# A hybrid layer with a mixture of experts: the sixteen tasks of the embedding gate put into units 4, 6 and 7, and a register read moved from unit 10 to unit 4

## The chip, the core and the metric

The kernel runs on one core of a Trainium2 chip. A core has TensorE (PE; its weight loads are listed apart as PEld), VectorE (DVE), ScalarE (ACT), GpSimd (POOL), SyncE (SP), which here issues all transfers, and 16 DMA engines. Each engine works through its own instructions in their order; semaphores tie them together. The metric is the device time of one execution in microseconds. A kernel's time is the median over its executions; the profile is one further execution with its own time.

## What is computed

One decoder layer on 512 tokens of width 1024, all in float32. Attention, convolution and the first norm lie ahead of the stage that matters here. Behind them comes

```python
ffn = hier_moe(x, w_router_g, b_router_g, w_router_e, b_router_e, w_gate, w_up, w_down)
ple = jax.nn.sigmoid(x @ w_ple_gate) * (p @ w_ple_proj)
x = layer_norm(ALPHA * x + ffn + ple, ln2_g, ln2_b)
```

`hier_moe` sends each token to 2 of 32 experts; an expert is `(silu(xb @ w_gate) * (xb @ w_up)) @ w_down` with two 1024 x 512 matrices and one 512 x 1024. `ple` is the embedding gate: a 1024 x 1024 product, a sigmoid, and a 256 x 1024 projection of `p`.

## The kernel before

**Units.** The experts are sorted by load and handled in twelve units: `KINDS = "PQPPQPPQPPQP"`. A P unit has two experts with 64 token slots each, a Q unit four with 32. A unit has eight gate steps (line 898: one step takes the 128 rows k of gate and up weights), the activation (902 to 904), a transpose of the hidden rows (909, 911), and four down steps (918). The weights come in pieces of 1 MiB, each two half pieces of 512 KB (`load_expert`, line 263); a P unit uses 12 pieces, a Q unit 24, two in each step. All weights are read once, so the stage moves about 200 MB.

**Slots.** All large buffers lie in 24 slots of 1 MiB (`Slots`). `pump` puts the loads of a fixed queue into the program as soon as a slot is free in program order; the instruction on SP waits until the matmuls that read the slot before are done. What other buffers hold, the weights can't use; "pieces ahead" are those issued beyond the step being computed.

**Filler.** Between the weight steps, `pace` fills in other work of TensorE from two lanes: scatters of the previous unit's output (930, eight pairs of matmuls), the selection matrices (890), gathers of the tokens for coming units (764), and the gate's tasks. A list of weights sets the share at each point: in a P unit most of it stands between the last gate step and the first down step; in a Q unit it is spread, with half of it in that place. This place is called a unit's pause below.

**The gate.** Its sixteen tasks are four chunks of 256 output columns (`w_pg`) times four tiles of 128 tokens. A task (`ple_task`) is 24 matmuls of 128 x 256 (132 to 134: the product as three products of rounded halves), two projections (743, two records each), a sigmoid on ACT (753), a product on DVE (754) and an addition on POOL (758). `PLE` says how many tasks a unit gets. The chunk's weights are loaded before the unit of the chunk's first task, and a chore in the unit ahead of it (`ple_chunk`) splits them on ACT and DVE into a pair of slots, which are given back behind the chunk's fourth task. The split token rows (four slots) and the projection's operands (one) are held from unit 2 to the last task.

**The overflow test.** If an expert has more tokens than its slots, a loop at the end of unit 10 handles the rest (`overflow`, line 961 on). Unit 2 counts the blocks into `nxi`; every engine reads the number into a register (961) and branches on it (962). Here nothing overflows. On SP the branch stands behind a wait for all issued loads; the last unit's last two pieces (line 270) are issued only behind it.

Of the kernel before, what the change touches and what calls it, by code (L numbers as in the profile page):

```python
# [19 lines left out]
T = 512  # L20
# [5 lines left out]
NE = 32  # L26
EPG = 8
FE = 512
CAP = 64
# [19 lines left out]
SEL = 1024.0  # L49
N_SLOTS = 24  # L50
WARM = 9
PLE = {4: 4, 6: 1, 7: 5, 9: 1, 10: 5}
WEIGHTS = {"P": [1.5, 0, 1.5, 0] + [5, 2.5] + [0, 1, 0], "Q": [2, 2, 2, 1.5] + [3, 2] + [1, 2, 1]}
LAST = [4, 0, 4, 0, 2, 2]

# [44 lines left out]
def hybrid_moe_layer_kernel(ctx: ExitStack, tc: tile.TileContext, xT, xtok, pT, w_in, w_conv, w_out, ln1, w_r,  # L100
                            b_r, w_e, w_last, w_pg, w_pp, ln2, cst, out):
    nc = tc.nc
# [8 lines left out]
    def ps(tag):  # L111
        return psum.tile([P, 512], F32, tag=tag, name=f"ps_{tag}", bufs=banks[tag])

    def sm(name, shape, dtype=F32, bufs=2):
        return spool.tile(list(shape), dtype, tag=name, name=name, bufs=bufs)
# [37 lines left out]
    def claim(key, shape, dtype=F32, urgent=False):  # L153

        (wants.appendleft if urgent else wants.append)((key, shape, dtype))
# [13 lines left out]
    def need(key):  # L169
        while key not in loaded:  # L170
            pump(slots.left() - 1)
        return loaded.pop(key)
# [72 lines left out]
    tasks = {}  # L245
    for n in sorted(PLE):
        t = sum(len(v) for v in tasks.values())
        tasks[n] = list(range(t, t + PLE[n]))
    rows_of, base = w_e.rearrange("n u p i d -> (n u p i) d"), {}
# [464 lines left out]
    def ple_start():  # L714

        for j in range(2):
            for i in range(2):
                claim((("x", j), i), [P, KD, 2 * P], F32R)
            yield from halve(("x", j), x1T[j])

    def ple_chunk(c):
        for i in range(2):
            claim((("pg", c), i), [P, KD, 256], F32R)
        yield (("pg", c), 1)
        yield from halve(("pg", c), need(("pg", c)))
# [3 lines left out]
    def ple_task(n):  # L729
        c, tt = divmod(n, NT)  # L730
        if n == 0:
            ple["pq"] = need(("pq",))
        pq = ple["pq"].t
        cc, ts = slice(c * 256, (c + 1) * 256), slice((tt % 2) * P, (tt % 2 + 1) * P)
        o = ps("s")
        held_bank[0] = True
        (xh, xl), (gh, gl) = ([b.t for b in ple[key]] for key in (("x", tt // 2), ("pg", c)))
        for k in range(KD):
            mm3(o[:, 0:256], xh[:, k, ts], xl[:, k, ts], gh[:, k], gl[:, k], k == 0, k == KD - 1)
            if k % 2:  # L740
                yield 0.65
        for k in range(2):
            nc.tensor.matmul(o[:, 256:512], pq[:, k * T + tt * P:k * T + (tt + 1) * P], proj_part(pq, c)[:, k],
                             start=(k == 0), stop=(k == 1))
        if tt == 3:
            slots.give(*ple["pg", c])
            if c < 2:
                load_proj(pq, c + 2)
            if c == 3:
                slots.give(ple["pq"], *(b for j in range(2) for b in ple["x", j]))  # L750
        yield 0.4
        s = sm("ps", [P, 256], bufs=1)
        nc.scalar.activation(s, o[:, 0:256], AF.Sigmoid)  # L753
        nc.vector.tensor_mul(s, s, o[:, 256:512])  # L754
        held_bank[0] = False
        yield 0.2
        r = row(tt)[:, cc]
        nc.gpsimd.tensor_tensor(r, r, s, op=ALU.add)  # L758
        yield 0.01
# [182 lines left out]
    nxi = cpool.tile([P, 1], I32, name="nxi")  # L942

    def find_blocks(keys):
        for b in range(1, NBLK):
            nc.vector.tensor_scalar(keys[:, b - 1], cnt, float(CAP * (b - 1)), None, op0=ALU.is_gt)

    def count_blocks():

        o = ps("z")  # L950
        for tt in range(NT):
            nc.tensor.matmul(o[:, 0:NE], onesb, mc[:, tt], start=(tt == 0), stop=(tt == NT - 1))
        nc.vector.tensor_sub(cnt, o[:, 0:NE], caps)
        keys = sm("hw", [P, FE], bufs=1)[:, 0:(NBLK - 1) * NE].rearrange("p (b e) -> p b e", e=NE)
        find_blocks(keys)
        nx = sm("nx", [P, 1])
        nc.vector.tensor_reduce(nx, keys, axis=AX.XY, op=ALU.add)
        nc.vector.tensor_copy(nxi, nx)

    def overflow():  # L960
        nv = nc.values_load(nxi[0:1, 0:1], min_val=0, max_val=2 * T // CAP + NE)
        with tc.If(nv > 0):
            own = list(slots.q)
            ws, wb, tb, kb = own[0:4]
# [1 line left out]
            n = (NBLK - 1) * NE  # L966
# [81 lines left out]
    def add(cost, gen, lane=1):  # L1048
        lanes[lane].append((cost, gen))
# [22 lines left out]
    def fill(share):  # L1072

        spare[0] += share * (rest(0) + rest(1))
        while (lanes[0] or lanes[1]) and spare[0] > 0:
            spare[0] -= any_piece()
        spare[0] = min(spare[0], 1.0)

    def drain():
        while lanes[0] or lanes[1]:  # L1080
            any_piece()
# [15 lines left out]
    def place_pair(n):  # L1097
        places[n] = t = sm("pt", [P, T], F32R, bufs=1)
        e, m, cap = UNITS[n]
        place(t, lambda tt: rmb[:, tt, e:e + m], m, cap)  # L1100
        yield 0.3
# [13 lines left out]
    for n in range(NU):  # L1115
        g, r = GROUP_OF[n]
        ne, cap = UNITS[n][1:]
        o = [ps("mm") for _ in range(2)]
        point = [0]

        def pace():
            w = (LAST if n == NU - 1 else WEIGHTS[KINDS[n]])[point[0]:]
            if w[0]:
                fill(w[0] / sum(w))
            point[0] += 1

        def pieces(u):
            return [need(("e", n, j, u)) for j in range(ne // 2)]

        if scat is not None:  # L1130
            add(3.6, scat, 0)
        add(0.3, place_pair(n), 0)
        done[:] = [0.0, 0.0]
        ahead = n == GROUPS[g][-1] and g + 1 < NG
        if ahead:
            claim(("xe", g + 1), [P, KD, GROUP], F32, True)
            if g % 2:
                claim(("pts", g + 1), [P, NT, 2 * GROUP], F32R, True)
        for t in tasks.get(n, []):
            add(3.5, ple_task(t))  # L1140
        if n + 2 == min(tasks):
            chores.append(ple_start())
        for t in tasks.get(n + 1, []):
            if t % NT == 0:
                chores.append(ple_chunk(t // NT))
        chore()
        for k in range(KD):
            bs = pieces(k)
            gate_up(o, k, [xe[g].t[:, k, r * P + i * cap:r * P + (i + 1) * cap] for i in range(ne)],
                    [b.t[:, i] for b in bs for i in range(2)])  # L1150
            slots.give(*bs)
            if n == NU - 1 and k == 1:
                closed.clear()
                slots.q.rotate(-4)
            serve()
            if k == 1 and ahead:
                select(g + 1)
                add(7.7 if len(GROUPS[g + 1]) > 1 else 5.3, gather_group(g + 1))
            if k > 0:
                chore()  # L1160
            if n == 0 and k == 2:
                late[0] = group_weights(0)
                next(late[0])
            if r == 0 and k == 4:
                for _ in late.pop(g):
                    pass
            if n == 2 and k == 6:
                count_blocks()
            if k % 2:
                pace()  # L1170
        h = sm("hw", [P, FE], bufs=1)
        swiglu(h, o, wsl[g][r], P)
        pace()
        ht = turn_hidden(h, P)
        pace()
        if n == NU - 1:
            drain()
            break
        o = [ps("y") for _ in range(2)]
        if n == 0:  # L1180
            for j in range(2):
                claim(("acc", j), [P, 2, D])
        for f in range(4):
            bs = pieces(8 + f)
            down(o, f, ht, [b.t[:, i] for b in bs for i in range(2)], cap)
            slots.give(*bs)
            if f == 3:
                claim("y", [P, 4 * T], F32R, True)
            serve()
            chore()  # L1190
            if f < 3:
                pace()
        y = grab("y")
        if n == NU - 2:
            overflow()
            closed.discard(("e", NU - 1, 0, 10))
            serve()
        for h in range(2):
            split_out(halves(y.t, h), o[h], P)
        scat = scatter_pair(n, y.t, y)  # L1200
        while chore():
            pass
        if n == NU - 2:
            drain()
        if n == GROUPS[g][-1]:
            drain()
            slots.give(xe.pop(g))

    n, y, sq, diag = NU - 1, slots.take([P, 4 * T], F32R), slots.take([P, 512]), slots.take([P, 2, P])
# [228 lines left out]
```

## Time and profile before

| | us |
|---|---|
| three executions | 794.64, 796.34, 797.72 |
| median | 796.34 |
| the profiled execution, its own time | 794.04 |
| its span | 792.3 |
| PE busy (share of the span) | 748.8 (95%) |
| DVE, ACT, POOL busy | 315.2, 163.0, 84.3 |
| bytes moved | 233.51 MB, mean 295 GB/s |

The span is what the profile shows from the first to the last instruction; 1.7 us of the execution's time lie around it. A matmul's end is modelled, so TensorE's busy share says little on whether it sets the pace; the bandwidth in slices and what SP waits for say more. The last gate step of each unit and the first down step behind it are found in the timeline of PE by their lines, 898 and 918.

### The profile page before, as it was taken

The numbers are of one execution on the slowest core, as the hardware profiler recorded it, in microseconds if no ns is written. First come the engines' busy times: TensorE is split into PE (matmuls) and PEld (weight loads), VectorE is DVE, ScalarE is ACT, GpSimd is POOL, SyncE is SP. The second block draws the span as 40 slices with busy tenths as digits, with TensorE's granted clock in tenths as the row PEclk, the third lists the DMA queues.
The fourth block names the chain that finished last, engine by engine and source line by source line (L and its number), as shares of the span: only waits on it lengthen the run. The fifth ranks groups of instructions, "written<-read, shape, count | busy, mean of one in ns | idle before, by whom it ended". The sixth has DMA issues, their size and how long they took to land. (4 is left out here: it accounts for less than half of the span.)

```text
span 792.3 us, 11610 instructions
## 1 busy us (share of the span) xinstructions
PE 748.8 (95%) x4322; PEld 445.2 (56%) x4323; DVE 315.2 (40%) x637; ACT 163.0 (21%) x337; POOL 84.3 (11%) x107
## 2 busy tenths in 40 slices
PE   8999999999978999899999999999999999999795
PEld 5887877888857452246334653364454634457242
DVE  3646544646695413445430324241123324012145
ACT  5545454232022020012100120110000111001024
POOL 0224254000142000000000100000000000000005
PEclk9999999999995799999999999999999999999997
DMA  8401301547810779999999999989999999999942
GB/s 310 191 1 31 130 1 54 213 160 302 342 45 1 286 299 356 409 409 405 408 409 408 409 406 410 409 352 335 409 408 407 412 408 408 408 409 408 354 161 106
DMA packets 63675, 233.51 MB, mean 295 GB/s; under 512 B 7040, under 2 KB 10752, under 8 KB 59264
## 3 DMA queue, kind: packets, MB, share of 16 engines
q1 hardware_dynamic: 63616, 232.74, 75.0%
q8 instruction: 35, 0.57, 0.3%
q14 instruction: 24, 0.20, 0.1%
HBM read 230.62 MB, written 2.10 MB: 294 GB/s over the span
## 5 line engine op out<-in xcount | busy, mean ns | idle before, releaser
L898 PE MATMUL ps_mm<-big,big 128*32 128x512 f32 (+1 forms) x1024 | 225.4, 608 | 14.3 <-DMA big<-in_w_e_dram 8.5
L898 PEld LDWEIGHTS ps_mm<-big,big 128*32 128x32 f32 (+1 forms) x1024 | 60.1, 124 | 152.2 <-issue 93.0
L132 PE MATMUL ps_mm<-big,big 128*128 128x512 f32 (+1 forms) x272 | 103.2, 379 | 3.1 <-ACT big L118 2.6
L133 PE MATMUL ps_mm<-big,big 128*128 128x512 f32 (+1 forms) x272 | 100.2, 368 | 0.0
L134 PE MATMUL ps_mm<-big,big 128*128 128x512 f32 (+1 forms) x272 | 99.8, 367 | 0.1
L918 PE MATMUL ps_y<-big,ht 128*32 128x512 f32 (+1 forms) x480 | 86.4, 598 | 0.9 <-DMA big<-in_w_e_dram 0.9
L939 DVE TENSOR_TENSOR big<-big,ps_s 128x512 f32<-128x512 f32 x80 | 52.7, 683 | 82.0 <-PE ps_s L930 81.5
L119 DVE TENSOR_TENSOR big<-big,big 128x512 fp32r<-128x512 f32 (+1 forms) x78 | 63.3, 843 | 37.6 <-ACT big L118 28.6
L118 ACT CAST big<-big 128x512 fp32r<-128x512 f32 (+1 forms) x78 | 54.5, 743 | 50.2 <-DVE big L429 20.1
L758 POOL TENSOR_TENSOR big<-big,ps 128x256 f32<-128x256 f32 x16 | 11.7, 733 | 461.5 <-DVE big L939 266.2
L930 PE MATMUL ps_s<-big,pt 128*128 128x512 f32 x176 | 59.2, 437 | 1.4 <-DVE big L939 0.8
L132 PEld LDWEIGHTS ps_mm<-big,big 128*128 128x128 f32 x272 | 51.8, 190 | 15.3 <-ACT big L118 3.7
L134 PEld LDWEIGHTS ps_mm<-big,big 128*128 128x128 f32 x272 | 51.7, 190 | 8.9 <-DVE big L119 0.4
L133 PEld LDWEIGHTS ps_mm<-big,big 128*128 128x128 f32 x272 | 51.7, 190 | 8.1 <-DVE big L119 0.5
L764 PEld LDWEIGHTS ps_s<-big,big 128*128 128x128 f32 x384 | 48.9, 189 | 10.4 <-issue 6.6
L764 PE MATMUL ps_s<-big,big 128*128 128x256 f32 (+1 forms) x384 | 52.3, 284 | 0.1
L918 PEld LDWEIGHTS ps_y<-big,ht 128*32 128x32 f32 (+1 forms) x480 | 22.7, 122 | 44.7 <-issue 35.7
L371 POOL TENSOR_SCALAR big<-big,rden 128x128 f32<-128x128 f32 (+3 forms) x32 | 39.1, 1232 | 71.1 <-DVE rden L369 71.1
L930 PEld LDWEIGHTS ps_s<-big,pt 128*128 128x128 f32 x176 | 29.4, 192 | 27.9 <-issue 17.3
L754 DVE TENSOR_TENSOR ps<-ps,ps_s 128x256 f32<-128x256 f32 x16 | 6.7, 421 | 90.3 <-ACT ps L753 90.3
L132 PE MATMUL ps_s<-big,big 128*128 128x256 f32 x128 | 37.3, 292 | 0.2
L133 PE MATMUL ps_s<-big,big 128*128 128x256 f32 x128 | 36.1, 282 | 0.0
(234 smaller groups left out, 736.9 us busy)
## 6 DMA issues: line engine op xcount, KB each, us to landing
big<-in_w_e_dram SPq DMA_DIRECT2D x360, 512.0 KB, 10.2
big<-in_w_e_dram SPq DMA_DIRECT2D x12, 1024.0 KB, 8.9
big<-in_w_in_dram SPq DMA_DIRECT2D x11, 1024.0 KB, 6.8
big<-in_w_out_dram SPq DMA_DIRECT2D x4, 1024.0 KB, 6.9
big<-in_w_pg_dram SPq DMA_DIRECT2D x4, 1024.0 KB, 11.1
big<-in_xtok_dram SPq DMA_DIRECT2D x2, 1024.0 KB, 6.9
out_dram<-big SPq DMA_DIRECT2D x8, 256.0 KB, 2.1
big<-in_xT_dram SPq DMA_DIRECT2D x3, 512.0 KB, 8.8
```

The lines of the kernel that those rows point to most:

```text
L118: nc.scalar.copy(hi, raw)
L119: nc.vector.tensor_sub(lo, raw, hi.bitcast(F32))
L132: nc.tensor.matmul(o, ah, bh, start=first, stop=False)
L133: nc.tensor.matmul(o, ah, bl, start=False, stop=False)
L134: nc.tensor.matmul(o, al, bh, start=False, stop=last)
L371: nc.gpsimd.tensor_scalar(pr[h][:, 0:ks], pr[h][:, 0:ks], rden[:, h:h + 1], None, op0=ALU.mult)
L758: nc.gpsimd.tensor_tensor(r, r, s, op=ALU.add)
L764: nc.tensor.matmul(o[:, 0:n], src[tt // 2].t[:, tt % 2, k * P:(k + 1) * P], pt(tt), start=(i == 0), stop=(i == 2 * NT - 1))
L898: nc.tensor.matmul(o[a][i * m:(i + 1) * m], x, w[:, a * FE:(a + 1) * FE], start=(k == 0), stop=(k == KD - 1))
L918: nc.tensor.matmul(o[h][r], ht[:, f, r], w[:, h * 512:(h + 1) * 512], start=(f == 0), stop=(f == 3))
L930: nc.tensor.matmul(o, pt[0:m, tt * P:(tt + 1) * P], y[i][0:m], start=(i == 0), stop=(i == 1))
L939: nc.vector.tensor_add(r, r, o)
```

## The change

Before, units 4, 6, 7, 9 and 10 have 4, 1, 5, 1 and 5 tasks; now units 4, 6 and 7 have 7, 1 and 8. The register read for the overflow test is made behind the third gate step of unit 4, on all engines; the branch stays where it is.

```diff
-PLE = {4: 4, 6: 1, 7: 5, 9: 1, 10: 5}
+PLE = {4: 7, 6: 1, 7: 8}
...
+    over = []
+
     def overflow():
-        nv = nc.values_load(nxi[0:1, 0:1], min_val=0, max_val=2 * T // CAP + NE)
+        nv = over[0]
         with tc.If(nv > 0):
...
             if n == 2 and k == 6:
                 count_blocks()
+            if n == 4 and k == 2:
+                over.append(nc.values_load(nxi[0:1, 0:1], min_val=0, max_val=2 * T // CAP + NE))
```

By the chunks: chunk 1 (tasks 4 to 7) is now loaded with chunk 0 ahead of unit 4 and split in unit 3 instead of 5; chunks 2 and 3 are loaded together ahead of unit 7 and both split in unit 6, where before chunk 3 came in unit 9. The queue of loads is otherwise the same, and no byte is added.

On ACT, unit 4 before, from the rounding of unit 3's output (924) to that of unit 4's. Each row of 753 closes one task, 902 stands behind the last gate step, 911 ahead of the first down step:

```order
L924 CAST big_3352<-ps_y 128x512 x2
L753 ACTIVATE ps<-ps_s 128x256 x3
L902 ACTIVATE hw<-ps_mm 128x512
L753 ACTIVATE ps<-ps_s 128x256
L911 COPY ht<-ps_z 128x512
L766 COPY big_3367<-ps_s 128x256 x4
L808 COPY w_3830<-ps_z 4x128 x2
L924 CAST big_3849<-ps_y 128x512 x2
```

In the change, the same stretch:

```order
L924 CAST big_3354<-ps_y 128x512 x2
L753 ACTIVATE ps<-ps_s 128x256
L1172 TENSOR_LOAD nxi
L753 ACTIVATE ps<-ps_s 128x256 x3
L902 ACTIVATE hw<-ps_mm 128x512
L753 ACTIVATE ps<-ps_s 128x256 x2
L911 COPY ht<-ps_z 128x512
L753 ACTIVATE ps<-ps_s 128x256
L766 COPY big_3369<-ps_s 128x256 x4
L808 COPY w_3940<-ps_z 4x128 x2
L924 CAST big_3959<-ps_y 128x512 x2
```

Between 902 and 911 two tasks are closed where one was, and another one behind 911, where there were only gathers (766).

On SP, ahead of unit 4's first weights, before (241 and 238 are the projection's operands, 148 the gate chunk, 260 and `ISA` work out the address of an expert):

```order
L263 DMA big_2837<-in_w_e_dram 128x1024
L241 DMA big_2840<-in_pT_dram 128x1024
L238 DMA big_2840<-in_w_pp_dram 128x2x256 x2
L148 DMA big_2872<-in_w_pg_dram 128x2048
L260 TENSOR_LOAD table
L260 ISA x2
L263 ISA
```

In the change:

```order
L263 DMA big_2837<-in_w_e_dram 128x1024
L241 DMA big_2840<-in_pT_dram 128x1024
L238 DMA big_2840<-in_w_pp_dram 128x2x256 x2
L148 DMA big_2872<-in_w_pg_dram 128x2048
L148 DMA big_2934<-in_w_pg_dram 128x2048
L260 TENSOR_LOAD table
L260 ISA x2
L263 ISA
```

A second chunk stands ahead of unit 4's weights and takes a slot from them.

## Rows read from the trace of the kernel before

**Rows 1.** The page, bandwidth in 40 equal slices of the span

```profile
GB/s 310 191 1 31 130 1 54 213 160 302 342 45 1 286 299 356 409 409 405 408 409 408 409 406 410 409 352 335 409 408 407 412 408 408 408 409 408 354 161 106
```

**Rows 2.** Table by stretch: us, length, five engines' busy time, clock, DMA share, GB/s

```profile
350.00:515.00 165.00, 159.09 (x868) 74.74 (x868) 51.96 (x106) 22.00 (x40) 2.93 (x4) 1.00 1.03 408
...
530.00:545.00 15.00, 15.00 (x106) 8.55 (x107) 4.95 (x8) 3.07 (x8) 0.00 (x0) 1.00 0.72 247
545.00:700.00 155.00, 151.07 (x874) 74.80 (x869) 39.09 (x80) 13.72 (x28) 5.35 (x8) 1.00 1.03 409
700.00:735.00 35.00, 34.68 (x272) 23.06 (x270) 7.81 (x16) 3.98 (x11) 2.71 (x4) 1.00 1.03 408
```

**Rows 3.** SP's waits, 509 to 546 us: total, times, longest

```profile
SPq L263 <- PE ps_s L930: 8.0, 1, 8.0
SPq L263 <- PE ps_mm L898: 6.8, 4, 2.3
```

**Rows 4.** SP's waits from 700 to 738 us, the same columns

```profile
SPq L263 <- DMA big<-in_w_e_dram: 18.2, 24, 1.3
```

**Rows 5.** Timeline of PE at unit 6's pause: start, length, instruction, count

```profile
522.49 1.89 PE L898 MATMUL ps_mm<-big,big 128*64 128x512 f32 x8
524.30 0.73 PE L930 MATMUL ps_s<-big,pt 128*128 128x512 f32 x2
524.88 1.10 PE L764 MATMUL ps_s<-big,big 128*128 128x256 f32 x8
525.81 0.63 PE L930 MATMUL ps_s<-big,pt 128*128 128x512 f32 x2
...
535.54 1.51 PE L918 MATMUL ps_y<-big,ht 128*64 128x512 f32 x6
```

**Rows 6.** Timeline of PE at unit 4's pause, with one whole task

```profile
443.63 1.90 PE L898 MATMUL ps_mm<-big,big 128*32 128x512 f32 x10 [0.23 <-DMA big<-in_w_e_dram]
...
448.33 0.28 PE L132 MATMUL ps_s<-big,big 128*128 128x256 f32 x1
...
451.21 1.03 PE L743 MATMUL ps_s<-big 128*128 128x256 f32 x4
451.88 1.28 PE L930 MATMUL ps_s<-big,pt 128*128 128x512 f32 x4
...
457.18 1.92 PE L918 MATMUL ps_y<-big,ht 128*32 128x512 f32 x16
```

**Rows 7.** Timeline of PE at unit 7's pause

```profile
578.75 1.91 PE L898 MATMUL ps_mm<-big,big 128*32 128x512 f32 x10 [0.24 <-DMA big<-in_w_e_dram]
...
590.40 1.92 PE L918 MATMUL ps_y<-big,ht 128*32 128x512 f32 x16
```

**Rows 8.** Timeline of PE at the end of unit 10

```profile
733.04 1.92 PE L918 MATMUL ps_y<-big,ht 128*32 128x512 f32 x16
740.29 1.97 PE L898 MATMUL ps_mm<-big,big 128*64 128x512 f32 x4 [5.33 <-PEq L962]
```

**Rows 9.** Timeline of SP, the last piece of unit 10 and what follows

```profile
718.31 1.47 SPq L263 DMA_DIRECT2D big<-in_w_e_dram  x2
```

**Rows 10.** DMA issues from 717.7 to 718.5 us: count, KB, us to landing

```profile
big<-in_w_e_dram SPq DMA_DIRECT2D x2, 512.0 KB, 7.8
```

**Rows 11.** Line 961 and line 962, PE's sequencer: min, median, max ns, start

```profile
L961 PEldq TENSOR_LOAD <-nxi x1: 488/488/488, 733.1 to 733.1; - x1
...
L962 PEldq COMPARE_BRANCH  x1: 6172/6172/6172, 733.7 to 733.7; - x1
```

**Rows 12.** Line 263, all weight loads but the last unit's end

```profile
DMA to landing us min/median/max: 3.2/10.2/13.0
```

**Rows 13.** Line 270, the last unit's loads, ns and first and last start

```profile
L270 SPq DMA_DIRECT2D big<-in_w_e_dram x8: 372/374/392, 738.8 to 756.4; - x8
```

**Rows 14.** DMA issues from 756.3 to 756.7 us

```profile
big<-in_w_e_dram SPq DMA_DIRECT2D x1, 512.0 KB, 7.8
```

**Rows 15.** Timeline of PE, the last unit's last down step

```profile
770.56 1.08 PE L1230 MATMUL ps_mm<-big,ht 128*64 128x256 f32 x8
```

## The prediction

> **What bounds the kernel now.** I read the page's slices first, for the stage in which the weight transfers run without a break. The bandwidth line stands at 400 to 412 GB/s in nearly all slices from the 16th on, with a dent to 352 and 335 and a fall at the end [rows 1]. The table by stretch puts the dent between 530 and 545 us: 247 GB/s there, against 408 and 409 before and behind it [rows 2]. So the expert stage is a stream of weight pieces at 1.049 MB / 408 GB/s = 2.57 us each, and it lost 15 x (1 - 247/408) = 5.9 us once. The waits of SP say why: in that stretch it waited 8.0 and 6.8 us for matmuls, that is, for buffers (slots) that TensorE had not yet freed [rows 3], while from 700 to 738 us it waited 18.2 us for the queue itself, which was full [rows 4]. The TensorE rows at unit 6 show the cause: between the last gate step (522.49 + 1.89 = 524.38) and the first down step (535.54) stand 11.2 us of filler, scatters and gathers [rows 5], and in that time no weight buffer comes free.
>
> The stage ends otherwise. The last piece of unit 10 is issued at 718.31 [rows 9] and such issues land after 7.8 us [rows 10], at 726.1. With the last down step behind it (1.92 us [rows 8]) unit 10 could end at 728.0; it ends at 733.04 + 1.92 = 734.96. TensorE is **7.0 us late** on the stream there. Then it stands still until 740.29 [rows 8], since its branch at the overflow test takes 6.17 us [rows 11].
>
> **The change, part by part.** Nothing is computed less. One gate task is 24 matmuls at (451.21 - 448.33)/24 = 0.12 us plus an end of 451.88 - 451.21 = 0.67 us, 3.55 us in all [rows 6]. Five of them (17.8 us) leave unit 10 and one leaves unit 9; three more go to unit 4 and three more to unit 7.
>
> *Slots.* Splitting a gate chunk makes a pair of buffers that stay until the chunk's fourth task. Before, chunk 1 is split in unit 5; now, with seven tasks in unit 4, in unit 3. Of 24 slots unit 4 held 17 (normalised rows 4, running sum 2, gathered inputs 2, selection 1, expert output 1, gate operand 4, projection 1, one pair 2), so two pieces were in use and five ahead. With a second pair it is three ahead.
>
> *Unit 4's pause.* Before, it runs from 443.63 + 1.90 = 445.53 to 457.18, 11.65 us [rows 6]; the order now has 78 task matmuls in it instead of 36, four ends instead of two, 8 gather matmuls instead of 24. With a gather of eight at 525.81 - 524.88 = 0.93 us [rows 5] that is 11.65 + 42 x 0.12 + 2 x 0.67 - 2 x 0.93 = 16.2 us. The stream has three pieces ahead, two that the last gate step frees, and two from chunk 0's pair: 7 x 2.57, and 0.6 us for a projection reload, 18.6 us. From the landing of the last gate piece to the first new bytes pass 1.9 (gate step) + 16.2 + 1.9 (first down step) + 1.9 us (the shortest issue to landing, 3.2 us [rows 12], less 1.3 us of transfer) = 21.9 us. **Dry: 3.3 us** at least. Unit 6 lost 5.9 us for a longest wait of 8.0, so wait less 2.1 us; here SP would wait from about 3.5 us into the pause (chunk 0's fourth task ends 6 x 0.12 + 0.67 = 1.4 us into it, and four half pieces go out behind that) to 16.2 + 1.9 = 18.1, which is 14.6 us, and lose 12.5 by that. Unit 4 enters with a full queue, unit 6 did not, so I stay near the floor: 6.0 (3.3 to 12.5). The same count on the old unit 4 (nine pieces, 23.1 us, against 17.4) gives no gap, and the trace has none. Between unit 4's gate steps there are now up to 4.9 us of filler (30 task matmuls, an end and a scatter of 524.88 - 524.30 = 0.58 us [rows 5]) with three pieces ahead: 1.5 us (0 to 2.5).
>
> *Unit 6.* Its filler stays. But chunk 3's raw weights now lie in a slot through its first gate steps, and chunk 3's pair takes the next two slots freed behind the last one, while chunk 1's pair comes free a little earlier. One piece more ahead would give 2.57 us back; a piece that waits for the first down step instead of the last scatter costs 2.8 us, and one fewer ahead 2.57 more. I take +3.0 (-2.6 to +5.4), the upper half, because SP's 6.8 us of short waits fall where a slot is now missing.
>
> *Unit 7.* The pause was 590.40 - (578.75 + 1.91) = 9.74 us [rows 7]; 30 matmuls and an end more make 14.0. Eight pieces (four ahead, two that the last gate step frees, two from a finished pair) last 20.6 us, needed are 1.9 + 14.0 + 1.9 + 1.9 = 19.7: no gap by the count, and with unit 4's excess (6.0 - 3.3) added, about 2.0 (0 to 4).
>
> *Units 8 to 10.* Here the gate's seven to nine slots are free, so 12 to 16 pieces are ahead and the stream doesn't break. It ends 6.0 + 1.5 + 3.0 + 2.0 = **12.5 us later** (0.7 to 24 with every bound at its end; 5 to 19 as I believe them).
>
> *The end.* Unit 10 without tasks waits for its weights, so TensorE's 7.0 us of lateness are gone: the unit ends 12.5 - 7.0 = 5.5 us later, and 0.5 us less by the register read that no longer stands ahead of the branch [rows 11]. On SP the overflow test lets everything land before the last four half pieces go out; the last goes at 756.4 [rows 13] and lands 7.8 us later [rows 14], at 764.2. Now that is 776.7, while TensorE wants it at 770.56 [rows 15] + 5.0 = 775.6. So the stream and not TensorE sets the end, by 776.7 - 770.56 = 6.1, **+6.2 us** with the 0.1 us from landing to matmul. The profiled execution of 794.04 us becomes 800.2, and on the median, which is 2.3 us above it, 796.34 + 6.2 = 802.5.
>
> *The register read in unit 4* costs nothing: 0.49 us on TensorE [rows 11] where it waits for weights, and its source was written in unit 2. If that cover were gone it is at most 0.5 us once. Left out: between 0 and 0.5.
>
> [...] The row shows the branch at 6.17 us and the read ahead of it at 0.49 [rows 11], so what is long is the jump and not the value. [...]
>
> **The rivals.** *The slots suffice (no change).* The stream loses only a few us more: unit 4 at its floor and unit 6 with a slot won. At 6 us lost the sum is 6 - 6.3, 796.0. For it: the count gives only 3.3 us for certain. Against: unit 6 of before lost 5.9 us with four pieces ahead.
>
> *The last units win (faster).* Place: the end of unit 10; price: up to 7.0 us of lateness, which vanish whatever happens. It decides if the stream loses under 2.3 us more: with 1 us it is 796.34 - 5.3 = 791.0. For it: unit 6's own gap could shrink by 2.6. Against: a pause of 16.2 us with 18.6 us in hand.
>
> *The early read takes the branch's stall away.* That would give 5.33 us back: 802.5 - 5.3 = 797.2, no change. It would need the jump to be known before it is reached. Against it is the row above: the read ended 0.1 us before the branch began and the wait is the branch's. A chance of 4 in 100.
>
> That the change does nothing is excluded by the order: the tasks stand where its numbers say.
>
> **How the numbers follow.** About 0.5%, 4 us, is what a measurement of this kernel can tell from no change. Slower by more needs a stream that loses over 10.3 us: forecast, 66 in 100, with 802.5. Between: 21 in 100 (17 for the slots, 4 for the branch). Faster: 13 in 100. The range runs from 795 (5 us lost) to 809 (19 us lost).
>
> **What would show it.** In the profile after: a new dent of bandwidth near 460 us, at unit 4's pause of about 16 us, with a long SP wait for matmuls; the dent of unit 6 still there, some 10 us later; a small one at unit 7; 408 GB/s from then on; TensorE waiting for weights in unit 10 and hardly any lateness at its end; the branch still at some 6 us. I am wrong if the bandwidth near 460 us holds, or if unit 6's dent is gone.

## The result, and the profile after

The changed kernel takes 801.21 us (median of seven executions, 800.5 to 804.86) against 795.9 us for the kernel before (also seven); the ratio is 1.0079, with a 95% interval of 1.0058 to 1.01. It is slower, by some 0.8%. The profiled execution took 800.5 us, its span 798.7 us; before they were 794.04 and 792.3.

The page's bandwidth in 40 slices, after; the line of before is in [rows 1]:

```profile
GB/s 305 191 1 50 109 1 54 212 158 316 366 3 1 311 319 367 408 408 408 408 409 373 406 309 404 412 346 294 409 409 351 409 408 409 408 410 408 404 214 105
```

One dent has become four: 373 and 309 GB/s (unit 4), 346 and 294 (unit 6), 351 (unit 7). Behind them 408 to 410, as before. The table by stretch says how much that is. Its columns are the stretch, its length, the busy time of PE, PEld, DVE, ACT and POOL, TensorE's granted clock, the DMA share and GB/s. First before:

```profile
420.00:480.00 60.00, 58.55 (x376) 30.94 (x370) 14.35 (x23) 7.09 (x15) 2.93 (x4) 1.00 1.03 408
480.00:560.00 80.00, 76.50 (x405) 36.05 (x405) 23.87 (x45) 8.67 (x17) 0.73 (x1) 1.00 0.97 377
560.00:640.00 80.00, 78.55 (x483) 42.46 (x484) 21.88 (x47) 8.07 (x19) 3.67 (x5) 1.00 1.03 408
```

and after:

```profile
420.00:460.00 40.00, 39.40 (x270) 26.67 (x269) 7.45 (x14) 3.11 (x8) 4.43 (x6) 1.00 1.01 390
460.00:480.00 20.00, 20.00 (x177) 13.53 (x177) 4.08 (x8) 2.65 (x9) 0.74 (x1) 1.00 0.83 309
480.00:560.00 80.00, 74.32 (x376) 35.19 (x375) 27.64 (x49) 11.76 (x21) 0.73 (x1) 0.96 0.95 364
560.00:640.00 80.00, 79.31 (x526) 46.49 (x527) 17.84 (x41) 6.41 (x14) 5.89 (x8) 1.00 1.01 395
640.00:740.00 100.00, 94.47 (x526) 38.89 (x525) 26.54 (x51) 9.03 (x21) 0.00 (x0) 1.00 1.03 409
```

A stretch lost its length times (1 - GB/s / 409). Before, that is 0.1 + 6.3 + 0.2 = 6.6 us between 420 and 640 us. After, it is 40 x 19/409 = 1.9 between unit 4's gate steps, 20 x 100/409 = 4.9 at its pause (460 to 480 us), 80 x 45/409 = 8.8 around unit 6 and 80 x 14/409 = 2.7 at unit 7: 18.3 us, **11.7 more**. From 460 to 480 us TensorE is busy throughout, at a granted clock of 1.00, while the stream stands still for a quarter of the time: in the pause the engine works, but on filler. The pieces issued ahead carry the stream almost to the pause's end; the standstill itself lies at that end and just behind it (330, 23 and 203 GB/s in the 2 us from 462, 464 and 466).

The clock's 0.96 around unit 6 comes from one place. TensorE waited 3.45 us for weights there, then the granted clock is 0.50 from 510 to 515 us (0.85 in the 5 us behind them), and fifteen matmuls of a gate step take 6.8 us where sixteen later ones take 3.65. What this adds to unit 6's loss no run separates.

SP's waits in two of the stretches of after, first 440 to 475 us (total, times, longest), then 598 to 616 us:

```profile
SPq L263 <- PE ps_y L918: 9.3, 2, 8.7
SPq L263 <- PE ps_mm L898: 5.3, 2, 5.0
...
SPq L263 <- PE ps_y L918: 6.9, 2, 6.2
```

In both, SP's longest wait is for the first down step (918) to free a slot; at the old dent it waited for matmuls too [rows 3]. TensorE's own rows give the pauses, unit 4's and then unit 7's, each from the last gate step to the first down step:

```profile
445.89 1.90 PE L898 MATMUL ps_mm<-big,big 128*32 128x512 f32 x10 [0.23 <-DMA big<-in_w_e_dram]
...
463.97 1.92 PE L918 MATMUL ps_y<-big,ht 128*32 128x512 f32 x16
...
590.65 1.90 PE L898 MATMUL ps_mm<-big,big 128*32 128x512 f32 x10 [0.23 <-DMA big<-in_w_e_dram]
...
606.43 1.92 PE L918 MATMUL ps_y<-big,ht 128*32 128x512 f32 x16
```

That is 463.97 - 447.79 = 16.2 us (11.65 before [rows 6]) and 606.43 - 592.55 = 13.9 us (9.74 before [rows 7]).

The end of unit 10 after, from its last gate step to its last down step, the branch, and the first step of unit 11:

```profile
717.00 1.90 PE L898 MATMUL ps_mm<-big,big 128*32 128x512 f32 x10 [0.24 <-DMA big<-in_w_e_dram]
...
736.19 1.05 PE L918 MATMUL ps_y<-big,ht 128*32 128x512 f32 x2 [0.22 <-DMA big<-in_w_e_dram]
737.47 1.90 PE L918 MATMUL ps_y<-big,ht 128*32 128x512 f32 x10 [0.23 <-DMA big<-in_w_e_dram]
744.14 4.53 PE L898 MATMUL ps_mm<-big,big 128*64 128x512 f32 x10 [4.77 <-PEq L964]
```

Before, the same last gate step began at 706.03 and the last down step stood there without a wait [rows 8]. Now the down steps wait for weights. From the last gate row to the start of the branch pass 737.51 - 717.00 = 20.5 us, where it was 733.66 - 706.03 = 27.6. The chain of waits that ended last (start, length, what) runs through a transfer near its end, that of the very last half piece; before, the chain of the last unit has no transfer in it:

```profile
766.86 8.14 DMA big<-in_w_e_dram
775.00 0.04 issue
775.04 1.08 PE ps_mm L1234 x6
```

### The profile page after: what moved, and what is told of

Same layout as the page of the kernel before. It is cut to its first block, busy times and chain, and to the rows that moved or that the text cites. A ratio compares the mean times of both kernels' runs of the same rounds, so it can differ in the third digit from the quotient of the medians.

```text
span 798.7 us, 11590 instructions
## 1 busy us (share of the span) xinstructions
PE 747.7 (94%) x4323; PEld 443.5 (56%) x4323; DVE 315.7 (40%) x637; ACT 163.6 (20%) x337; POOL 84.4 (11%) x107
## 5 line engine op out<-in xcount | busy, mean ns | idle before, releaser
L898 PE MATMUL ps_mm<-big,big 128*32 128x512 f32 (+1 forms) x1024 | 222.0, 614 | 17.6 <-DMA big<-in_w_e_dram 12.6
L898 PEld LDWEIGHTS ps_mm<-big,big 128*32 128x32 f32 (+1 forms) x1024 | 58.3, 125 | 154.6 <-issue 98.1
L918 PE MATMUL ps_y<-big,ht 128*32 128x512 f32 (+1 forms) x480 | 90.6, 613 | 1.4 <-DMA big<-in_w_e_dram 1.4
L132 PEld LDWEIGHTS ps_mm<-big,big 128*128 128x128 f32 x272 | 51.3, 189 | 16.2 <-ACT big L118 4.8
L764 PEld LDWEIGHTS ps_s<-big,big 128*128 128x128 f32 x384 | 49.4, 189 | 11.6 <-issue 7.4
L758 POOL TENSOR_TENSOR big<-big,ps 128x256 f32<-128x256 f32 x16 | 11.8, 737 | 362.1 <-DVE ps L754 186.3
L132 PE MATMUL ps_s<-big,big 128*128 128x256 f32 x128 | 37.4, 292 | 0.0
L925 DVE TENSOR_TENSOR big<-ps_y,big 128x512 fp32r<-128x512 f32 (+1 forms) x24 | 15.7, 677 | 52.9 <-ACT big L924 52.5
```

The lines of the kernel that those rows point to most:

```text
L132: nc.tensor.matmul(o, ah, bh, start=first, stop=False)
L764: nc.tensor.matmul(o[:, 0:n], src[tt // 2].t[:, tt % 2, k * P:(k + 1) * P], pt(tt), start=(i == 0), stop=(i == 2 * NT - 1))
L898: nc.tensor.matmul(o[a][i * m:(i + 1) * m], x, w[:, a * FE:(a + 1) * FE], start=(k == 0), stop=(k == KD - 1))
L918: nc.tensor.matmul(o[h][r], ht[:, f, r], w[:, h * 512:(h + 1) * 512], start=(f == 0), stop=(f == 3))
L925: nc.vector.tensor_sub(y[1][0:m], o[0:m], y[0][0:m].bitcast(F32))
```

## The experiments

Their results are ratios to the kernel before, run between them on the same chip, with 95% intervals.

**The read alone.**

```diff
 (kernel before)
+            if n == 4 and k == 2:
+                over.append(nc.values_load(nxi[0:1, 0:1], ...))
...
-        nv = nc.values_load(nxi[0:1, 0:1], ...)
+        nv = over[0]
```

> The kernel before with only the register read moved from unit 10 to unit 4. Theory: the read was never late and the 6.17 us behind the branch's row are not its doing, so the time stays within -0.6 to +0.3 us of the 795.9 us before, and the COMPARE_BRANCH row of TensorE's sequencer still lasts 6.0 to 6.3 us. Rival: the read next to the branch is what makes the branch slow; then the branch's row shrinks below 1 us, and TensorE, whose unit 11 begins that much earlier, ends up to 5.3 us sooner (down to 790.6 us, less if the last transfers then bind).

Measured: 794.73 against 795.32 us, 0.9992 (0.9977 to 1.0007). TensorE's branch:

```profile
L964 PEldq COMPARE_BRANCH  x1: 6062/6062/6062, 731.2 to 731.2; - x1
```

The branch takes what it took next to the read [rows 11]. The read is no part of the result, and the rival of the early read falls.

**The table alone.**

```diff
-PLE = {4: 4, 6: 1, 7: 5, 9: 1, 10: 5}
+PLE = {4: 7, 6: 1, 7: 8}
```

> The changed kernel's table (7 tasks in unit 4, 1 in unit 6, 8 in unit 7) with the register read left in unit 10. Theory: the table is the whole of the change, so the time is that of the changed kernel, 801.2 us, within 0.6 us (the read's 0.49 us on TensorE comes back next to the branch), +5.3 to +5.9 us over the kernel before, and the same stretches without traffic at 460 to 475, 525 to 555 and 605 to 620 us. Rival: the early read, with TensorE's halt of 0.49 us in the middle of unit 4, takes part in the dry spell there; then this kernel is more than 1.5 us faster than the changed one.

Measured: 802.19 us, 1.0078 (1.0056 to 1.01), where the whole change has 1.0079. By the medians it is 6.9 us over the kernel before, where 5.3 to 5.9 were expected; by the ratios the two agree. The table is the change, and the rival (the early read takes part in the dry spell) falls.

**Unit 4's part alone.**

```diff
-PLE = {4: 4, 6: 1, 7: 5, 9: 1, 10: 5}
+PLE = {4: 7, 6: 1, 7: 2, 9: 1, 10: 5}
```

> The kernel before with three tasks moved from unit 7 to unit 4 (7, 1, 2, 1, 5 in units 4, 6, 7, 9, 10) and the read as before: unit 10 keeps its five tasks. Theory (lost stream time sets the end): unit 4's pause grows to 16 us, the weight stream falls dry there for 4 to 7 us, unit 6's old dry spell grows by up to 3 us and unit 7's pause shrinks below the old 9.7 us; of some 6 us lost in all, the time grows by 3.5 to 5.6 us (799.4 to 801.5). Rival (TensorE's work in unit 10 sets the end, whatever the stream does): the five tasks still stand in unit 10, so the time stays within 1 us of 795.9.

Measured: 798.0 us, 1.0033 (1.0021 to 1.0045), +2.7 us. The table by stretch of this kernel:

```profile
420.00:480.00 60.00, 59.41 (x439) 40.35 (x441) 11.52 (x22) 5.67 (x15) 5.17 (x7) 1.00 0.94 357
480.00:560.00 80.00, 77.92 (x430) 37.01 (x422) 25.88 (x48) 9.75 (x19) 0.73 (x1) 1.00 1.03 408
560.00:640.00 80.00, 76.92 (x413) 34.00 (x414) 20.53 (x43) 6.21 (x14) 1.46 (x2) 1.00 1.02 409
```

Unit 4 loses 60 x 52/409 = 7.6 us, by itself. The rival (unit 10's work decides, whatever the stream does) falls: five tasks stand in unit 10 and the time still grows. But the expectation of 3.5 us and more was missed, because unit 6, which was to lose more, lost **nothing** (480 to 560 us). Its pause is as long as ever, 11.6 us. What differs is that chunk 1 is finished in unit 6 and chunk 3 is not split until unit 9, so one pair of slots is held in unit 6's pause and not two. This pointed to slots more than any run before it. The loss in these three stretches is only some 1.1 us more than before, less than the 2.7 us of time. Unit 10's last gate row starts 1.9 us later and the way from it to the branch is 0.8 us longer (the table below); from 700 to 740 us this kernel's stream moves 395 GB/s for 408, with SP waiting 3.5 us for a task of unit 10 (2.7 before). What made that end longer stays open.

**Everything into unit 7.**

```diff
-PLE = {4: 4, 6: 1, 7: 5, 9: 1, 10: 5}
+PLE = {4: 4, 6: 1, 7: 11}
```

> The kernel before with unit 9's and unit 10's six tasks moved to unit 7 (4, 1, 11 in units 4, 6, 7) and the read as before. Theory (what counts is how many tasks stand in one unit's pause and how many slots are free there): unit 4 stays as it was, with no dry spell, unit 7's pause grows to 18 to 20 us, the stream loses 20 to 25 us there and at unit 6's place, and the time grows by 9 to 16 us (805 to 812), more than the changed kernel's +5.3, though nothing stands in unit 10 either. Rival (a task costs the same wherever it stands ahead of unit 10, so only their sum counts): about the changed kernel's time, 801.2 within 1.5 us.

Measured: 809.37 us, 1.0171 (1.0149 to 1.0193), +14 us. The rival (a task costs the same wherever it stands) falls. From 480 to 640 us:

```profile
480.00:560.00 80.00, 72.85 (x347) 33.39 (x346) 25.66 (x46) 10.77 (x19) 0.73 (x1) 0.96 0.87 330
560.00:640.00 80.00, 78.30 (x543) 52.15 (x544) 17.34 (x41) 6.46 (x15) 8.09 (x11) 1.00 0.93 352
```

Most of the loss, 80 x 79/409 = 15.5 us, is not at unit 7, where the tasks are, but around unit 6, whose filler is unchanged: there chunks 1, 2 and 3 now hold three pairs.

**Unit 10's tasks made light.**

```diff
 (kernel before, ple_task)
-            mm3(o[:, 0:256], ..., k == 0, k == KD - 1)
+            if n < 11 or k == 0:
+                mm3(o[:, 0:256], ..., k == 0, n >= 11 or k == KD - 1)
```

> The kernel before with unit 10's five gate tasks cut to 3 of their 24 main matmuls each (the gate's sums over 7 of 8 slices of the width are left out there, 5 x 21 x 0.12 = 12.6 us of TensorE); loads, slots and order stay. Theory: TensorE was 7.0 us late at unit 10's end, and what bounds it after that is the stream, whose last half piece is issued at 756.4 us and lands some 13 us later; so only a part of the 12.6 us comes back, 5 to 7 us (789 to 791). Rival 1: TensorE is the bound to the end, then the whole 12.6 us come back (783). Rival 2: the stream bound already, then the time stays within 1 us.

Measured: 790.98 us, 0.9936 (0.9916 to 0.9955), 4.4 us by the medians, 5.1 by the ratio. Both rivals fall: neither all 12.6 us come back, nor none. The size is at the lower end or just under it. (The expectation lets the last half piece land 13 us after its issue. The row says 7.8 [rows 14], at 764.2, some 6.4 us ahead of the last down step, so the range of 5 to 7 us stands.) TensorE's wait in the last unit, which the kernel before doesn't have, says what binds then:

```profile
PE ps_y L1231 <- DMA big<-in_w_e_dram: 2.1, 2, 1.2
```

**The same tasks, a shorter pause.**

```diff
 (the changed kernel, weights of a unit of four experts)
-"Q": [2, 2, 2, 1.5] + [3, 2] + [1, 2, 1]
+"Q": [3, 3, 3, 2] + [2, 1] + [2, 3, 2]
```

> The changed kernel with other weights for the units of eight experts (3, 3, 3, 2 for the gate-up steps, 2, 1 around the turn, 2, 3, 2 for the down steps, in place of 2, 2, 2, 1.5, 3, 2, 1, 2, 1): the same tasks in the same units, but more of each unit's extra work between its steps and less of it in its pause. Theory (the pause in which no weight slot is given back is what runs the stream dry): pauses of units 4 and 7 shrink by 3 to 5 us, the dry spells there by as much, and the time falls by 4 to 8 us against the changed kernel (793 to 797). Rival (the amount of work per unit counts, not where in the unit it stands): no change, 801.2 within 1 us.

(This expectation and those further down call the units of two and four experts units of four and eight. The old list puts 6.5 of its 16.5 parts into the pause of a unit of four experts, two fifths and not half of the filler; the new one 5 of 21.)

Measured: 794.14 us, 0.9988 (0.9971 to 1.0004): some 7 us less than the changed kernel, back at the time before. The rival (the amount of work per unit counts, not its place) falls. Unit 4's pause falls from 16.2 to 9.7 us. The table, 420 to 460, 460 to 480, and unit 7:

```profile
420.00:460.00 40.00, 39.73 (x278) 27.34 (x277) 7.04 (x13) 3.38 (x8) 4.42 (x6) 1.00 0.98 368
460.00:480.00 20.00, 20.00 (x176) 13.56 (x176) 4.08 (x8) 2.19 (x6) 0.73 (x1) 1.00 1.03 408
600.00:640.00 40.00, 40.00 (x266) 23.47 (x263) 12.80 (x27) 3.81 (x9) 2.22 (x3) 1.00 1.03 408
```

The pause of unit 4 loses nothing now; between the gate steps 4.0 us are lost where it was 1.9. What was taken out of the pause was partly given back there, and still 7 us were won.

**The same tasks and pauses, more slots.**

```diff
 (the changed kernel; one rounded half of the gate's operands)
-            for i in range(2):
-                claim((("x", j), i), [P, KD, 2 * P], F32R)
+            claim((("x", j), 0), [P, KD, 2 * P], F32R)
...
-            mm3(o[:, 0:256], xh[:, k, ts], xl[:, k, ts], gh[:, k], gl[:, k], k == 0, k == KD - 1)
+            mm3(o[:, 0:256], xh[:, k, ts], xh[:, k, ts], gh[:, k], gh[:, k], k == 0, k == KD - 1)
```

> The changed kernel with the gate's low halves left out of its operands (the high halves are used in their place, so that every task keeps its 24 matmuls and its duration; the gate's rounding is coarser, and VectorE's subtractions for the low halves are gone): 2 slots in place of 4 for the tokens and 1 in place of 2 for each chunk of the gate's weights, 3 to 4 slots more for the weight stream in units 4 to 7. Theory (slots held by the gate's operands are why the stream can't run through the longer pauses): the pauses stay at 16 and 14 us, but the dry spells at 460 to 475, 525 to 555 and 605 to 620 us shrink from 16.3 us together to under 5, and the time falls by 10 to 18 us against the changed kernel (783 to 791). Rival (the stream stalls for what stands in the way of its issue or transfer, not for slots): the dry spells stay and the time is within 2 us of 801.2.

Measured: 786.41 us, 0.9884 (0.9865 to 0.9904), nearly 15 us under the changed kernel. The pauses of units 4, 6 and 7 are the same, 16.2, 11.6 and 13.9 us, and the stream doesn't break:

```profile
420.00:480.00 60.00, 59.40 (x445) 39.91 (x445) 11.88 (x23) 6.62 (x17) 5.17 (x7) 1.00 1.03 408
480.00:560.00 80.00, 79.55 (x461) 41.10 (x456) 24.17 (x48) 11.04 (x21) 1.46 (x2) 1.00 1.03 409
560.00:640.00 80.00, 79.72 (x538) 48.47 (x538) 21.80 (x47) 8.12 (x19) 5.16 (x7) 1.00 1.03 408
```

TensorE does the same number of matmuls in the same places; with three to four slots more, 0.3 us are lost of the 18.3. (The kernel leaves the low halves of the gate's operands out, so its gate is coarser, and VectorE's subtractions for them are gone too. But SP waited for matmuls, and VectorE ended none of its long waits in the changed kernel: 0.2 us from 500 to 550 us. The next run touches slots alone.)

**One slot held empty.**

```diff
 (kernel before)
+        if n == 5:
+            claim("hold", [P, KD, 256])
+        if n == 8:
+            slots.give(got.pop("hold"))
```

> The kernel before with one slot of the 24 held empty from unit 5 to the start of unit 8; tasks, order of the work and read as before. Theory (slots are what the stream lacks in the pauses): one piece fewer ahead costs 2.57 us wherever the stream already runs dry, so unit 6's dry spell grows from 6 us to 8 to 9 us, some 1 us more is lost between gate steps of unit 6, and unit 10 ends 2.5 to 4.5 us later; time +2 to +4.5 us (797.5 to 800). Rival (the dry spell is a matter of the pause's length alone, the slots are ample): unit 6's dry spell stays at 6 us and the time within 1 us of 795.4.

Measured: 799.03 us, 1.0039 (1.0019 to 1.0059), +4 us; the rival falls.

```profile
480.00:560.00 80.00, 75.89 (x391) 35.85 (x394) 24.25 (x46) 8.67 (x17) 0.73 (x1) 1.00 0.93 353
```

80 x 56/409 = 11.0 us are lost there where it was 6.3: **4.7 us for one slot**, nearly two transfers of 2.57 us. Two kernels above have the same units 4 to 9 as the kernel before and show how well this repeats: the read alone lost 7.0 us there (373 GB/s) and the light unit 10 lost 7.4 (371), so one slot cost 3.6 to 4.7 us. The pause lost hardly more than before; the rest went between the gate steps ahead of it, where SP now waited 8.2 us for them instead of 6.8 [rows 3].

**Four ways to place the tasks better.** They need no more than the numbers of the table and the weights.

```diff
-PLE = {4: 4, 6: 1, 7: 5, 9: 1, 10: 5}
+PLE = {4: 4, 7: 8, 9: 2, 10: 2}
```

> The kernel before with the tasks as 4, 8, 2, 2 in units 4, 7, 9 and 10, the read as before. Theory: unit 4 keeps its four tasks and so no dry spell, unit 6 loses its one, the gate's third and fourth chunk of weights are claimed later, unit 10 keeps two tasks that TensorE carries without being late (3 x 3.55 = 10.7 us less than before against the 7.0 us it was late); the stream loses some 2 us more than before: time falls by 3 to 6 us (790 to 793). Rival (eight tasks in unit 7 run the stream dry there as in the changed kernel, by 2.8 us and more): no gain, within 1.5 us of 795.9.

Measured: 792.29 us, 0.9954 (0.9939 to 0.997), as expected, and the rival falls. The stream lost 7.1 us, 0.5 more than before, where 2 were expected.

The same tasks with flatter weights:

```diff
+WEIGHTS = {"P": [2.5, 0, 2.5, 0] + [4, 2] + [0, 1, 0], "Q": [3, 3, 3, 2.5] + [2, 1.5] + [1, 2, 1]}
```

> Tasks as 4, 8, 2, 2 in units 4, 7, 9 and 10, and flatter weights in both kinds of unit (four experts: 2.5, 0, 2.5, 0 for the gate-up steps, 4, 2 around the turn, 0, 1, 0 for the down steps; eight experts: 3, 3, 3, 2.5, then 2, 1.5, then 1, 2, 1). Theory: the pauses shrink by 2 to 4 us, unit 6's dry spell loses 1 to 3 us of its 6, and the time falls by 2 to 3 us below the same tasks with the old weights, to 788 to 790. Rival (work put between gate steps delays the freeing of slots there as much as the pause gives): no difference to the 792.3 us of the old weights.

Measured: 789.12 us, 0.9928 (0.991 to 0.9946). The time is as expected, the reason isn't: unit 6's pause fell from 8.6 us in the kernel ahead to 6.5, and yet 6.3 us were lost there (480 to 560 us: 377 GB/s) where that one lost 5.7. The two intervals overlap and the spans of the two profiled executions are alike (786.8 and 787.0), so it is open whether these weights gave anything.

```diff
-PLE = {4: 4, 6: 1, 7: 5, 9: 1, 10: 5}
+PLE = {4: 5, 7: 7, 9: 2, 10: 2}
...
-"Q": [2, 2, 2, 1.5] + [3, 2] + [1, 2, 1]
+"Q": [3, 3, 3, 2] + [2, 1] + [2, 3, 2]
```

> Tasks as 5, 7, 2, 2 in units 4, 7, 9 and 10, the weights of four-expert units as before and those of eight-expert units flatter (3, 3, 3, 2, then 2, 1, then 2, 3, 2). Theory: as with 6, 6, 2, 2: 5 to 8 us of stream time lost in all, unit 10 short, 787 to 790 us. Rival: the fifth task in unit 4 opens a second pair there and costs a dry spell of 3 to 6 us, 792 or more.

Measured: 789.14 us, 0.9915 (0.9897 to 0.9932), as expected; the rival (a second pair in unit 4 makes it 792 or more) falls.

```diff
-PLE = {4: 4, 6: 1, 7: 5, 9: 1, 10: 5}
+PLE = {4: 6, 7: 6, 9: 2, 10: 2}
...
+WEIGHTS = {"P": [2.5, 0, 2.5, 0] + [4, 2] + [0, 1, 0], "Q": [3, 3, 3, 2] + [2, 1] + [2, 3, 2]}
```

> Tasks as 6, 6, 2, 2 in units 4, 7, 9 and 10, with flatter weights (four experts: 2.5, 0, 2.5, 0, then 4, 2, then 0, 1, 0; eight experts: 3, 3, 3, 2, then 2, 1, then 2, 3, 2). Theory: six tasks in unit 4, spread over its steps, keep its dry time at 0 to 4 us, and with chunk 1 finished in unit 7's first tasks unit 6 loses 2 to 4 us where it lost 6; 7 us lost in all or fewer, unit 10 as short as with two tasks: 787 to 790 us. Rival (unit 4 can't carry more than four tasks): its dry spell of 6 us comes back and the time is 793 or more.

Measured: **786.81 us, 0.9893** (0.9874 to 0.9911). It beats both kernels and computes the same; its rival falls. From 420 to 560 us:

```profile
420.00:480.00 60.00, 58.52 (x426) 36.60 (x426) 11.72 (x22) 6.24 (x16) 4.43 (x6) 1.00 1.01 394
480.00:560.00 80.00, 78.18 (x427) 37.30 (x426) 25.42 (x47) 8.68 (x17) 0.73 (x1) 1.00 1.02 399
```

Lost are 2.2 and 2.0 us, and unit 10 keeps two tasks at the price of one us, as the table below shows.

Unit 6 has the same weights and the same pause, 6.5 us, as in 4, 8, 2, 2 with flatter weights, and two pairs are held there in both, yet 2.0 us were lost where it was 6.3. What SP waits for from 505 to 560 us tells the two kernels apart; 4, 8, 2, 2 comes first:

```profile
SPq L263 <- PE ps_y L918: 9.9, 3, 7.9
...
SPq L263 <- PE ps_s L930: 3.5, 2, 3.3
```

In 4, 8, 2, 2, chunks 1 and 2 are both split in unit 6, their pairs claim slots there ahead of the weights, and the next piece waits for the first down step. In 6, 6, 2, 2, chunk 1 was split in unit 3, only chunk 2 takes slots in unit 6, and the longest wait for a slot ends with a scatter inside the pause.

## Why the prediction was right

Predicted were 802.5 us, 6.2 more than before, slower; measured 801.21, 5.3 more by the medians and 6.4 more in the profiled executions. The sum had two terms with opposite signs, and the ten kernels of this table show both. "Lost" is the stream's loss between 420 and 640 us by the tables (in some rows over shorter stretches, which moves the last digit), "gate" the start of unit 10's last gate row, "tail" the time from there to the branch, all in us:

| kernel | tasks in unit 10 | lost | gate | tail | branch starts |
|---|---|---|---|---|---|
| before | 5 | 6.6 | 706.0 | 27.6 | 733.7 |
| unit 4 alone | 5 | 7.7 | 707.9 | 28.4 | 736.3 |
| one slot held | 5 | 11.8 | 712.1 | 27.6 | 739.7 |
| 4, 8, 2, 2 | 2 | 7.1 | 705.7 | 21.5 | 727.2 |
| 5, 7, 2, 2 | 2 | 6.6 | 705.0 | 22.1 | 727.1 |
| 6, 6, 2, 2 | 2 | 4.2 | 702.3 | 21.5 | 723.8 |
| after | 0 | 18.3 | 717.0 | 20.5 | 737.5 |
| after, shorter pause | 0 | 11.9 | 711.8 | 20.5 | 732.3 |
| after, more slots | 0 | 0.3 | 700.1 | 21.0 | 721.1 |
| all in unit 7 | 0 | 26.7 | 725.3 | 21.1 | 746.5 |

The gate column follows the lost column within 1.3 us (taken as differences to before). One kernel that the table leaves out doesn't: the read alone lost 7.4 us, 0.8 more than before, and its last gate row starts at 704.1, 1.9 us sooner. That execution reached the experts sooner: the last gate step of its first unit ends at 314.53, before at 316.72. So a gate or a branch time by itself says nothing under some 2 us. The tail is 27.6 to 28.4 us with five tasks and 20.5 to 21.1 with none, and two tasks are nearly free (21.5 to 22.1). What the stream lost repeats within some 1.2 us: 6.6, 7.4 and 7.8 in the three kernels whose units 4 to 9 are those of before (the last is the light unit 10), 18.3 and 18.2 in the two with the changed table.

- *TensorE 7.0 us late at unit 10's end*, with the read's 0.5 ahead of the branch 7.5: right, 27.6 - 20.5 = 7.1 us, and what is left of unit 10 waits for weights in its down steps.
- *Unit 4's pause 16.2 us*: 16.2. *Dry 6.0 there, near the floor*: 4.9, closer to the floor of 3.3 still. *Between the gate steps 1.5*: 1.9.
- *Unit 6 +3.0*: 8.8 against 6.3 for 480 to 560 us, +2.5. The size is not firm: by the kernels that repeat these units, 7.6 (the table alone) and 7.0 and 7.4 (the read alone, the light unit 10), it lies anywhere from +0.2 to +2.5. The reason given, chunks 2 and 3 both taking slots, is what the runs bear out. SP's longest wait was for a scatter (930), 8.0 us [rows 3], and is now, from 520 to 556 us, for the first down step, as the sum had it:

```profile
SPq L263 <- PE ps_y L918: 10.6, 2, 9.7
```

  With one pair 0.2 us are lost there (unit 4 alone), with two 6.3 (before), with three 15.5 (all in unit 7), and nothing in the changed kernel once each pair is a single slot. The number of pairs is not all, since it also counts where they are split (6, 6, 2, 2 above). The reason for the upper half of the range, that SP's 6.8 us of short waits would grow, was not borne out: its waits for gate steps are 4.2 us in that window.
- *Unit 7's pause 14.0 us, 2.0 lost*: 13.9 and 2.7.
- *In all 12.5 us later*: 11.7 lost; unit 10's last gate step is 11.0 us later.
- *Unit 10's end +5.0*: +3.85 (733.66 to 737.51). The stream's term was 1.5 us too large at that place.
- *The stream sets the end, +6.2*: the chain runs through the last unit's transfers, and the span grew by 6.4 us. SP's last issue moved from 756.4 [rows 13] to 766.9 us, 10.5 where 12.5 were predicted, and the transfer on the chain took 8.14 us for 7.8 [rows 14]. TensorE's last down step moved from 770.56 [rows 15] to 777.43, by 6.9. So the last stage added 2.6 us to unit 10's 3.85, where 1.2 were to be added to 5.0: two errors that cancel, and that the span's 6.4 lies so near to 6.2 is luck.
- *The register read at nothing*: right, by the first experiment, at 0.9992.
- *The branch keeps its stall*: 6.16 us after, and 6.06 in the kernel with the read alone. An early value changed nothing, which agrees with the prediction's reading of the row, that the jump is long and not the value; what the jump waits for no run shows.

What was only argued before and is now shown is that slots are the cause: more slots at equal pauses take nearly the whole loss away, and one slot fewer at equal pauses adds to it. What the prediction had too low is the price of a slot: it reckoned 2.57 us for a piece fewer ahead, and the slot held empty cost 3.6 to 4.7 us of stream time. That unit 4 came out near its floor may have hidden this.

## What to carry to other kernels

When a stage is bound by a stream of transfers, filler is priced by the buffers it holds and by the time in which it lets none be freed, more than by its own duration (here a slot held empty cost 3.6 to 4.7 us of the stream, and three to four slots more took its loss from 18.3 us to 0.3): count for each stretch without a release how many transfers are in hand, and put the filler where that number is high, spread over several places. Filler at the end of the stage costs only what outlasts the last transfer (two tasks about one us here, five tasks 7), so emptying that place altogether bought nothing beyond the first steps. Look too at which release the next transfer waits for: a buffer claimed ahead of it can push it from a release inside the filler to one behind it (in unit 6 the longest wait was 3.3 us for a scatter in 6, 6, 2, 2 and 7.9 us for a down step in 4, 8, 2, 2 with flatter weights). If moving work makes one place better, look for the buffers that open earlier because of it: the dearest loss can lie in a unit whose work was not touched (15.5 us around unit 6 with everything in unit 7).

## What the hardware showed that was not expected

TensorE alone pays for the branch at the overflow test. In the changed kernel the same branch takes 45 ns on POOL, 50 on ACT, 72 on DVE and 53 on SP. On TensorE:

```profile
L964 PEldq COMPARE_BRANCH  x1: 6157/6157/6157, 737.5 to 737.5; - x1
```

It took 6.17 us before, 6.06 with the read alone and 6.15 in 6, 6, 2, 2, wherever the read stood. In eleven kernels the first step behind it waited 4.6 to 5.5 us for it. The one where it waited less, 3.1 us, is the kernel with light tasks in unit 10, which has 105 matmuls fewer ahead of the branch:

```profile
L963 PEldq COMPARE_BRANCH  x1: 3930/3930/3930, 731.7 to 731.7; - x1
```

Why it was 2.2 us shorter there no run shows. The way from that kernel's last gate row (708.5) to the branch is 23.2 us, 4.4 us less than before, so the lighter tasks had their effect ahead of the branch; behind it TensorE waited 2.1 us for weights. What the shorter branch added to that experiment's 4.4 us is not shown.
